# Hybrid attention, convolution and memory layer: one buffer for both parts of a transposed group, a third scan buffer, two gates on the score banks, two sums of squares in one, other loads and stores at the two ends

## The chip, the cores and the metric

The kernel runs on one core of a Trainium2 chip. The metric is the device time of one execution in microseconds (us), as the median of several runs. PE is the matrix engine (PEld its weight loads), DVE the vector engine, ACT the scalar engine, POOL the GpSimd engine, SP the engine that starts most DMA transfers. Matmuls read SBUF and write PSUM, which has eight banks of 128 x 512 floats; DVE and ACT read both memories, POOL and DMA are used on SBUF alone here.

## The reference

One layer, `x` of 1024 tokens by 1024 features, 256 memory tokens. Cut to what is computed:

```python
h = rmsnorm(x, g_in)
q, k, v, u, b, c, q_mem, gate = split(h @ w_in)       # 3584 columns
# stick-breaking attention, 8 heads of 64, strictly causal (s < t), no softmax
z = q @ k.T / 8
w = sigmoid(z) * prod over s < j < t of (1 - sigmoid(z[t, j]))
y_sb = w @ v
y_conv = b * causal_conv3(c * u)                      # 256 channels
m_k, m_v = split(rmsnorm(mem, g_mem) @ w_mem_kv)
y_mem = softmax(q_mem @ m_k.T / 8) @ m_v              # 4 heads of 64
y = concat(rmsnorm(y_sb), rmsnorm(y_conv), rmsnorm(y_mem))
x = x + (y * silu(gate)) @ w_out
out = rmsnorm(x, g_final)
```

## The kernel before

Tokens are held in reverse order, so that the product over later keys becomes a scan to the right. Everything that goes into a matmul is split into a high part in fp32r (a cast on ACT) and a low part (what the cast left, a subtraction on DVE or POOL), and a product is three matmuls (high by high, high by low, low by high), or two where one side is stacked.

The work, in the order in which it is written down:

- At the start `xT` comes in by eight row blocks (`xs`), is scaled by `g_in` (in `col`, the first DMA on SP) and split into `xh`, `xl`. Eight warming matmuls on a zero mask run first on PE, then the first half of the values and the projections of the first heads.
- `proj(n, ...)` makes 128 columns of a projection: weights loaded and split (`load_w`, tags `whi` and `wlo`, four half tiles each), 48 matmuls of 128 x 512 into two banks with tag `pj`, and for each bank an `evac`.
- `sb_head` is one attention head. For each pair of token blocks `scores` makes the scores in banks `z`, ACT takes two sigmoids of them, DVE scans the product (into a buffer `F`), and DVE or POOL multiplies the scan with the sigmoid into `sg`. `apply` transposes four blocks of `sg` on PE into a bank `tr`; `transposed` casts the bank to the high part (`wth`, ACT) and subtracts for the low part (`wtl`, DVE), and two matmuls by the values add up in a bank `av`.
- `mem_head` is one memory head: scores in a bank `z`, softmax with Exp on ACT, the same transposes.
- `stats(c)` sums the squares of one of the eight tiles `ys[c]` (two halves: a Square, the split, two matmuls by a column of ones, a copy, four small DMAs that turn the row into a column). Tiles 0 to 3 are attention, 4 and 5 convolution, 6 and 7 memory.
- `gate(c)` is a projection whose `evac` multiplies by the row scale (DVE), takes a Sigmoid (ACT, written back to the bank), multiplies with the tile (DVE or POOL) and ends with a multiplication that reads the bank again and writes `y` (DVE). Only this last one sets the bank free.
- The output product takes eight blocks of 128 tokens. Each has three groups of matmuls, for the convolution's tiles 4 and 5 (banks `pj`), the memory's 6 and 7 (banks `z`) and the attention's 0 to 3 (banks `tr`, `av`); DVE adds each, scaled by its group's rms, to `acc`. Then comes the final norm: a Square with a sum on ACT, a power on POOL, a scaling of one half on DVE and of the other on ACT, two stores on SP. The last block takes its last 512 columns in two pieces of 256.

No order is written by hand. The functions above only record operations with a priority; a planner (`Plan.lay_out`) then lays them on the five engines, by costs of its own, always taking the ready operation of least priority, and issues the instructions in that order. Projections are fillers of low urgency between the steps of attention. A tag with n buffers gives them out in the order in which its tiles were written down, and a buffer comes free when all users of its tile are done. `nc.either` lets the planner choose DVE or POOL. All instructions are issued by one line, so every row of the profile says L383, and rows are told apart by the names of tiles.

Of the kernel before, what the change touches and what calls it, by code (L numbers as in the profile page):

```python
# [24 lines left out]
F32 = mybir.dt.float32  # L25
F32R = mybir.dt.float32r
BF16 = mybir.dt.bfloat16
AF = mybir.ActivationFunctionType
ALU = mybir.AluOpType
AX = mybir.AxisListType  # L30

P = 128
# [354 lines left out]
def hymba_kernel(ctx, tc, xT, xr, wp, wv, memT, memr, wmem, cols, eye, wout, gfin, out):  # L387
# [6 lines left out]
    vyp = Pool(nc, "vyp", {"va": 1, "vb": 1, "y0": 1, "y1": 1})  # L394
    att = Pool(nc, "att", {"qh": 1, "ql": 1, "kh": 1, "kl": 1, "q": 2, "qs": 2, "k": 2, "sg0": 2, "sg1": 2, "F": 2, "wth": 3, "wtl": 2})
    small = Pool(nc, "small", {"avt": 1, "mx": 2, "sm": 2, "part": 2})
# [5 lines left out]
    def bank(tag):  # L402
        return psum.tile([P, H], F32, tag)
# [4 lines left out]
    def one(shape, dt, name):  # L408
        return const.tile(shape, dt, name, name)

    def f(ap):
# [35 lines left out]
    nc.vector.tensor_copy(ones, onesf)  # L447
    nc.sync.dma_start(out=col, in_=cols)
    warm = one([P, 2], F32, "warm")
# [14 lines left out]
    for k in range(KC):  # L464
# [5 lines left out]
        if k % 2 == 0:  # L470
            ws = stage([P, 2, 256])
            wh, wl = att.tile([P, 2, 256], F32R, "wth", "wsh"), att.tile([P, 2, 256], F32R, "wtl", "wsl")
            nc.sync.dma_start(out=ws, in_=wv[0, k // 2])
# [113 lines left out]

    def proj(n, evac, after=(), both=False):
        fills[0] += 1
        wh, wl = load_w(wp[n], [P, KC, P], 8.4 if fills[0] == 1 else None)  # L590
        ps = [bank("pj"), bank("pj")]
        steps = [(i, k) for i in range(2) for k in range(KC)]
        if both:

            steps = [(i, k) for k in range(KC) for i in range(2)]
        for i, k in steps:
            hf = HALVES[i]
            for a, (ww, xx) in enumerate(((wh, xh), (wh, xl), (wl, xh))):
                first = k == 0 and a == 0
                nc.tensor.matmul(ps[i], lhsT=ww[k], rhs=xx[k][:, hf], start=first,  # L600
                                 stop=(k == KC - 1 and a == 2), prio=FILL + fills[0] + (0 if both else 0.4 * i),
                                 after=after if first else ())
            if k == KC - 1:
                keep, nc.prio = nc.prio, EVAC + fills[0]
                evac(ps[i], hf)
                nc.prio = keep
# [6 lines left out]
    def transposed(blocks):  # L613

        tr = bank("tr")
        for i, blk in enumerate(blocks):
            nc.tensor.transpose(tr[:, i * P : (i + 1) * P], blk, ident)
        wh = att.tile([P, H], F32R, "wth")
        wl = att.tile([P, H], F32R, "wtl")
        n = len(blocks) * P  # L620
        nc.scalar.copy(wh[:, 0:n], tr[:, 0:n])
        nc.vector.tensor_tensor(wl[:, 0:n], tr[:, 0:n], f(wh[:, 0:n]), op=ALU.subtract)
        return wh, wl
# [9 lines left out]
    def scores(st, sp, b):  # L633
# [5 lines left out]
        for c0, c1 in ((lo, min(n, H)), (H, n)):  # L639
            if c1 <= c0:  # L640
                continue
            z = bank("z")
            m0 = c0 if c1 - c0 >= 256 else c1 - 256
            for s, qq in enumerate((st["q"], st["qs"])):
# [102 lines left out]

    def stats(c, late=False):


        keep, nc.prio = nc.prio, EVAC + 50
        g = 0 if c < 4 else 1 if c < 6 else 2
        part = small.tile([P, TB], F32, "part")
        for n, hf in enumerate(HALVES):

            s, hi, lo = ((att if late else stg).tile([P, H], dt, tag if late else "stg", "sq")
                         for dt, tag in ((F32, "F"), (F32R, "sg1"), (F32R, "sg1")))
            nc.scalar.activation(s, ys[c][:, hf], AF.Square)
            nc.scalar.copy(hi, s)
# [44 lines left out]

    def gate(c, after, both=False):
        def evac(ps, hf):
            gz, y = stage(), ys[c][:, hf]
            nc.vector.tensor_tensor(gz, ps, rb[:, hf], op=ALU.mult)
            nc.scalar.activation(ps, gz, AF.Sigmoid)
            nc.either.tensor_tensor(gz, gz, y, op=ALU.mult)  # L810
            nc.vector.scalar_tensor_tensor(y, ps, gout(c), gz, op0=ALU.mult, op1=ALU.mult)

        proj(16 + c, evac, after, both)

# [134 lines left out]
    stats(5, late=True)  # L949
    gate(5, ())  # L950
    stats(6, late=True)
    gate(6, (last[6],))
    stats(7, late=True)
    gate(7, (), both=True)
    nc.prio = POST
# [29 lines left out]
    for j in range(TB):  # L985
# [18 lines left out]
        for n, c0, c1 in todo:  # L1004
# [9 lines left out]
            if n == todo[-1][0]:  # L1014
                junk = att.tile([P, H], F32, "F", "junk")
                nc.scalar.activation(junk[:, 0 : c1 - c0], acc[:, c0:c1], AF.Square,
                                     accum_out=sj[:, c0 // 256 : c0 // 256 + 1])
                if c0 == 0:
                    nc.vector.tensor_tensor(acc[:, 0:H], acc[:, 0:H], gf[:, 0:H], op=ALU.mult)
# [5 lines left out]
        nc.vector.tensor_tensor(acc[:, H:], acc[:, H:], gf[:, H:], op=ALU.mult)  # L1025
        nc.vector.tensor_scalar(acc[:, HALVES[0]], acc[:, HALVES[0]], total, None, op0=ALU.mult)
        nc.scalar.activation(acc[:, HALVES[1]], acc[:, HALVES[1]], AF.Copy, scale=total)
        for hf in HALVES:
            nc.sync.dma_start(out=out[j][:, hf], in_=acc[:, hf])
    nc.emit()  # L1030
# [49 lines left out]
```

## Time and profile before

| what | value |
|---|---|
| time, median of 3 runs | 561.36 us (561.23 to 561.88) |
| time of the profiled execution | 565.04 us |
| its span, first to last instruction | 563.3 us |
| PE busy (matmuls) | 548.9 us, 97%, 2984 instructions |
| PEld busy (weight loads, beside the matmuls) | 468.1 us |
| DVE busy | 404.5 us, 72% |
| ACT busy | 359.7 us, 64% |
| POOL busy | 179.8 us, 32% |
| mean granted clock of PE | 0.996 |
| read from and written to HBM | 36.78 MB and 4.20 MB |

A row of the timeline has the start, the time taken, engine, line, operation, out<-in, the shape and, in brackets, the idle time of the engine before it and what ended that. The time of one matmul is from its start to the end of its drain, and the next one starts long before that end; what a matmul costs a PE that is never idle is the distance between two starts.

### The profile page before, as it was taken

How to read it: one execution, taken by the hardware profiler on the slowest of the kernel's cores; microseconds unless marked ns; L12 is line 12 of the kernel's file. 1: busy time of each engine (PE TensorE's matmuls, PEld its weight loads, DVE VectorE, ACT ScalarE, POOL GpSimd, SP SyncE). 2: the span in 40 equal slices, each digit the busy share in tenths (PEclk: the TensorE clock that was granted, in tenths of full speed). 3: DMA queues.
4: the chain of work that ended last, by engine and by line, in shares of the span. 5: the costliest groups of instructions: out<-in, count | busy, mean ns of one | idle time of the engine just before them, and what ended most of it. 6: DMA issues, size and time to landing. Idle time of an engine off the chain costs nothing.

```text
span 563.3 us, 8740 instructions
## 1 busy us (share of the span) xinstructions
PE 548.9 (97%) x2984; PEld 468.1 (83%) x2984; DVE 404.5 (72%) x657; ACT 359.7 (64%) x727; POOL 179.8 (32%) x214
## 2 busy tenths in 40 slices
PE   6999999999999999999999999999999999999995
PEld 4898789998888888888888868888888777888884
DVE  3354588879888898973487879667777877876674
ACT  4843478788786777683278787766589975332322
POOL 1130154225444432452053474331442108010010
PEclk9999999999999999999999999999999999999998
DMA  7962915052142710115742512342522342223302
GB/s 238 389 188 75 234 42 131 21 111 78 40 92 60 184 39 19 39 21 120 197 151 76 131 38 75 75 104 71 164 76 38 114 149 76 74 76 115 110 37 75
DMA packets 34688, 58.36 MB, mean 104 GB/s; under 512 B 13650, under 2 KB 14546, under 8 KB 34644
## 3 DMA queue, kind: packets, MB, share of 16 engines
q1 hardware_dynamic: 34644, 57.81, 36.7%
q8 instruction: 23, 0.38, 0.3%
q14 instruction: 21, 0.17, 0.1%
HBM read 36.78 MB, written 4.20 MB: 73 GB/s over the span
## 4 chain that ended last, share of the span: by engine, by line
PE 88%; DMA 3%; ACT 3%; issue 2%; DVE 2%; POOL 1%; SPq 0%; POOLq 0%; DVEq 0%; ACTq 0%
PE pj L383 50%; PE tr L383 15%; PE z L383 12%; PE av L383 11%; DMA xs<-in_xT 1%; DMA wraw<-in_wmem 1%; DMA q<-ql 1%; DVE stg L383 0%; ACT L383 0%; ACT vh L383 0%; DVE y L383 0%; POOL wlo L383 0%; ACT z L383 0%; ACT pj L383 0%; ACT whi L383 0%
## 5 line engine op out<-in xcount | busy, mean ns | idle before, releaser
L383 PE MATMUL pj<-xh,whi 128*128 128x512 f32 x352 | 139.4, 396 | 0.7 <-DVE y L383 0.7
L383 PE MATMUL pj<-xh,wlo 128*128 128x512 f32 x352 | 139.8, 397 | 0.0
L383 PE MATMUL pj<-xl,whi 128*128 128x512 f32 x352 | 139.4, 396 | 0.0
L383 POOL TENSOR_TENSOR sg<-sg,F 128x512 f32<-128x512 f32 (+5 forms) x60 | 62.0, 1041 | 74.3 <-DVE F L383 47.8
L383 PEld LDWEIGHTS pj<-xh,whi 128*128 128x128 f32 x352 | 66.2, 188 | 13.2 <-DVE y L383 1.0
L383 PEld LDWEIGHTS pj<-xh,wlo 128*128 128x128 f32 x352 | 66.2, 188 | 12.3 <-issue 0.3
L383 PEld LDWEIGHTS pj<-xl,whi 128*128 128x128 f32 x352 | 66.2, 188 | 12.1 <-issue 0.2
L383 ACT ACTIVATE sg<-z,rq 128x511 f32<-128x511 f32 (+2 forms) x96 | 55.9, 583 | 29.8 <-PE z L383 27.0
L383 POOL TENSOR_TENSOR wlo<-wraw,whi 128x512 fp32r<-128x512 f32 x36 | 48.3, 1343 | 83.3 <-ACT whi L383 71.4
L383 DVE TENSOR_TENSOR_SCAN F<-z,mask 128x512 f32<-128x512 f32 (+2 forms) x64 | 60.1, 947 | 13.1 <-ACT z L383 10.9
L383 DVE TENSOR_TENSOR wtl<-tr,wth 128x512 fp32r<-128x512 f32 (+1 forms) x96 | 58.8, 639 | 5.8 <-ACT wth L383 5.0
L383 ACT CAST wth<-tr 128x512 fp32r<-128x512 f32 (+1 forms) x96 | 49.4, 552 | 15.4 <-PE tr L383 14.8
L383 ACT ACTIVATE z<-z,nrq 128x512 f32<-128x512 f32 (+3 forms) x96 | 53.4, 557 | 2.3
L383 PE MATMUL tr<-ident,sg 128*128 128x128 f32 x288 | 48.9, 273 | 0.0
L383 ACT CAST whi<-wraw 128x512 fp32r<-128x512 f32 x56 | 34.1, 621 | 14.9 <-PE pj L383 11.1
L383 PE MATMUL av<-wth,vh 128*128 128x256 f32 (+1 forms) x160 | 42.7, 276 | 0.0
L383 PE MATMUL av<-wtl,vh 128*128 128x256 f32 (+1 forms) x160 | 41.4, 293 | 0.0
L383 PEld LDWEIGHTS tr<-ident,sg 128*128 128x128 f32 x288 | 34.6, 140 | 2.9 <-DVE sg L383 0.2
L383 ACT ACTIVATE junk<-acc 128x512 f32<-128x512 f32 (+1 forms) x17 | 10.3, 606 | 38.9 <-DVE acc L383 38.1
L383 DVE TENSOR_TENSOR_SCAN F<-z,F,mask 128x511 f32<-128x511 f32 (+1 forms) x32 | 32.3, 1009 | 3.0 <-ACT z L383 1.5
L383 PE MATMUL z<-k,q 128*128 128x512 f32 (+2 forms) x96 | 34.0, 356 | 0.4 <-DMA q<-ql 0.4
L383 PEld LDWEIGHTS av<-wth,vh 128*128 128x128 f32 x160 | 30.3, 189 | 3.3
(173 smaller groups left out, 1206.2 us busy)
## 6 DMA issues: line engine op xcount, KB each, us to landing
wraw<-in_wp SPq DMA_DIRECT2D x44, 256.0 KB, 3.0
rows<-in_xr SPq DMA_DIRECT2D x8, 512.0 KB, 8.5
acc<-in_xr SPq DMA_DIRECT2D x8, 512.0 KB, 3.3
out<-acc SPq DMA_DIRECT2D x16, 256.0 KB, 2.1
xs<-in_xT SPq DMA_DIRECT2D x6, 512.0 KB, 9.2
q<-qh SPq DMA_DIRECT2D x12, 256.0 KB, 3.0
q<-ql SPq DMA_DIRECT2D x12, 256.0 KB, 4.6
qs<-ql SPq DMA_DIRECT2D x12, 256.0 KB, 4.7
```

The lines of the kernel that those rows point to most:

```text
L383: f(*[real(x) for x in o.args], **{k: real(x) for k, x in o.kw.items()})
```

## The change

- `transposed` takes the high and the low part from one tile with tag `wt`, two buffers of 128 x 2 x 512. Before, the high part had three buffers (`wth`) and the low part two (`wtl`). The weights of the first values (`wsh`, `wsl`) move to the same tag.
- The scans' tag `F` has three buffers where it had two.
- `scores` no longer widens a stretch of 128 keys to 256. That stretch occurs once in each of the eight attention heads (the last pair of blocks, second block), with two matmuls.
- `stats` takes several tiles of one group: it adds the squares of the second to those of the first (DVE or POOL) and sends the sum through one split, one set of matmuls and one set of small DMAs. It is called for tiles 6 and 7 together, after tile 7 is there.
- `proj` and `gate` take a tag for their two banks; the gates of tiles 5 and 7 use `z`.
- `col` is loaded from ACT's queue instead of SP's.
- In the last block of the output the Square of the last 256 columns is a multiplication with a sum on DVE instead of an ACT operation, and the scaling and the stores are four pieces (256 columns DVE, 192 ACT, 256 DVE, 320 ACT), the last store issued by ACT.

```diff
-    att = Pool(nc, "att", {..., "F": 2, "wth": 3, "wtl": 2})
+    att = Pool(nc, "att", {..., "F": 3, "wt": 2})
...
-    nc.sync.dma_start(out=col, in_=cols)
+    nc.scalar.dma_start(out=col, in_=cols)
...
-            wh, wl = att.tile([P, 2, 256], F32R, "wth", "wsh"), att.tile([P, 2, 256], F32R, "wtl", "wsl")
+            wh, wl = pair_of(att.tile([P, 2, 2, 256], F32R, "wt", "ws"))
...
-    def proj(n, evac, after=(), both=False):
+    def proj(n, evac, after=(), both=False, tag="pj"):
...
-        ps = [bank("pj"), bank("pj")]
+        ps = [bank(tag), bank(tag)]
...
-        wh = att.tile([P, H], F32R, "wth")
-        wl = att.tile([P, H], F32R, "wtl")
+        wh, wl = pair_of(att.tile([P, 2, H], F32R, "wt"))
...
-            m0 = c0 if c1 - c0 >= 256 else c1 - 256
+            m0 = c0
...
-    def stats(c, late=False):
+    def stats(*cs, late=False):
...
-            nc.scalar.activation(s, ys[c][:, hf], AF.Square)
+            nc.scalar.activation(s, ys[cs[0]][:, hf], AF.Square)
+            if len(cs) > 1:
+                t = (att if late else stg).tile([P, H], F32, "F" if late else "stg", "sq")
+                nc.scalar.activation(t, ys[cs[1]][:, hf], AF.Square)
+                nc.either.tensor_tensor(s, s, t, op=ALU.add)
...
-    gate(5, ())
-    stats(6, late=True)
+    gate(5, (), tag="z")
+    stats(6, 7, late=True)
     gate(6, (last[6],))
-    stats(7, late=True)
-    gate(7, (), both=True)
+    gate(7, (), both=True, tag="z")
...
-                nc.scalar.activation(junk[:, 0 : c1 - c0], acc[:, c0:c1], AF.Square,
-                                     accum_out=sj[:, c0 // 256 : c0 // 256 + 1])
+                if c1 - c0 < H and c1 == D:
+                    nc.vector.scalar_tensor_tensor(junk[:, 0 : c1 - c0], acc[:, c0:c1], 1.0, acc[:, c0:c1], op0=ALU.mult,
+                                                   op1=ALU.mult, accum_out=sj[:, c0 // 256 : c0 // 256 + 1])
+                else:
+                    nc.scalar.activation(junk[:, 0 : c1 - c0], acc[:, c0:c1], AF.Square,
+                                         accum_out=sj[:, c0 // 256 : c0 // 256 + 1])
...
-        nc.vector.tensor_scalar(acc[:, HALVES[0]], acc[:, HALVES[0]], total, None, op0=ALU.mult)
-        nc.scalar.activation(acc[:, HALVES[1]], acc[:, HALVES[1]], AF.Copy, scale=total)
-        for hf in HALVES:
-            nc.sync.dma_start(out=out[j][:, hf], in_=acc[:, hf])
+        for n, c in enumerate((slice(0, 256), slice(H, H + 192), slice(256, H), slice(H + 192, D)) if j == TB - 1 else HALVES):
+            if n % 2:
+                nc.scalar.activation(acc[:, c], acc[:, c], AF.Copy, scale=total)
+            else:
+                nc.vector.tensor_scalar(acc[:, c], acc[:, c], total, None, op0=ALU.mult)
+            (nc.scalar if n == 3 else nc.sync).dma_start(out=out[j][:, c], in_=acc[:, c])
```

Since tags, costs and banks feed the planner, the order changes on all engines. Three places matter for the prediction.

On PE, at the passage from the last gate to the output product, before: `pj_5336` is the second bank of the last gate (tile 7), `z_5412` and `z_5421` are banks of the group of tiles 6 and 7, `tr_5430` and `tr_5433` those of the attention's group, `pj_5451` the first bank of tiles 4 and 5, which takes over a bank of the last gate.

```order
L383 MATMUL pj_5336<-xh_448,wlo_5187 128x512
L383 MATMUL z_5412<-woh_5368,yh_4860 128x512
...
L383 MATMUL z_5421<-woh_5368,yl_4885 128x512
L383 MATMUL tr_5430<-woh_5398,yh_4860 128x512
L383 MATMUL tr_5433<-woh_5398,yh_4860 128x512
...
L383 MATMUL tr_5433<-woh_5426,yh_4860 128x512
L383 MATMUL pj_5451<-woh_4721,yh_4860 128x512
```

The same place in the changed program: `z_5223` is now the last gate's second bank, `z_5348` the first of the output product that takes over a bank of that gate.

```order
L383 MATMUL z_5223<-xh_444,wlo_5159 128x512
L383 MATMUL pj_5296<-woh_4631,yh_4767 128x512
...
L383 MATMUL pj_5309<-woh_5233,yl_4791 128x512
L383 MATMUL tr_5322<-woh_5272,yh_4767 128x512
...
L383 MATMUL tr_5338<-wol_5311,yh_4767 128x512
L383 MATMUL z_5348<-woh_5244,yh_4767 128x512
```

Between the last gate's last matmul and the first one that needs a bank of that gate stood 14 matmuls; now there are 24.

On PE at the gates before that, in the changed program: `z_5123` is the second bank of tile 5's gate, `pj_5001` the second bank of tile 6's, `z_5185` the first of tile 7's, `av_5183` the sums of squares.

```order
L383 MATMUL z_5123<-xh_444,wlo_4741 128x512
L383 MATMUL pj_5001<-xh_404,wlo_4930 128x512
L383 MATMUL pj_5001<-xh_444,whi_4921 128x512
L383 MATMUL pj_5001<-xl_453,whi_4921 128x512
L383 MATMUL pj_5001<-xh_444,wlo_4930 128x512
L383 MATMUL av_5183<-sq_5168,ones_99 2x512
L383 MATMUL z_5185<-xh_121,whi_5039 128x512
```

Before, the gates of tiles 3, 5, 6 and 7 followed each other on the same two `pj` banks; now tile 6's gate runs ahead of tile 5's, and 21 matmuls stand between the end of `z_5123` and the first matmul of the bank that takes over from it. The four `pj` matmuls at the end of tile 6's gate come late, after all of tile 5's.

On DVE the end of the program before (`acc` the last block, `ssf` the sums):

```order
L383 SCALAR_TENSOR_TENSOR acc_5914<-av_6086,rg_4451,acc_5914 128x256
L383 TENSOR_TENSOR ssf_5520<-ssf_5520 128x1
L383 TENSOR_TENSOR acc_5914<-acc_5914,gf_5134 128x512
L383 TENSOR_SCALAR acc_5914<-acc_5914,ssf_5520 128x512
L1075 UNCONDITIONAL_BRANCH
```

And after:

```order
L383 SCALAR_TENSOR_TENSOR acc_5790<-av_5962,rg_4366,acc_5790 128x256
L383 SCALAR_TENSOR_TENSOR junk_5981,ssf_5402<-acc_5790 128x256
L383 TENSOR_TENSOR ssf_5402<-ssf_5402 128x1
L383 TENSOR_TENSOR acc_5790<-acc_5790,gf_4988 128x512
L383 TENSOR_SCALAR acc_5790<-acc_5790,ssf_5402 128x256 x2
```

The last sum of squares now stands on DVE between the last addition and the total, and the scaling is two pieces. SP then has three stores instead of two, and ACT ends with a DMA of 128 x 320.

More of the change, by code (lines that the diff above doesn't have):

```diff
@@ L394, in hymba_kernel @@
     vyp = Pool(nc, "vyp", {"va": 1, "vb": 1, "y0": 1, "y1": 1})
-    att = Pool(nc, "att", {"qh": 1, "ql": 1, "kh": 1, "kl": 1, "q": 2, "qs": 2, "k": 2, "sg0": 2, "sg1": 2, "F": 2, "wth": 3, "wtl": 2})
+    att = Pool(nc, "att", {"qh": 1, "ql": 1, "kh": 1, "kl": 1, "q": 2, "qs": 2, "k": 2, "sg0": 2, "sg1": 2, "F": 3, "wt": 2})
     small = Pool(nc, "small", {"avt": 1, "mx": 2, "sm": 2, "part": 2})
@@ L409, in one, with pair_of @@
         return const.tile(shape, dt, name, name)
+    def pair_of(t):
+        return t[:, 0], t[:, 1]
     def f(ap):
@@ L746, in hymba_kernel @@
     summed = set()
-    def stats(c, late=False):
+    def stats(*cs, late=False):
         keep, nc.prio = nc.prio, EVAC + 50
-        g = 0 if c < 4 else 1 if c < 6 else 2
+        g = 0 if cs[0] < 4 else 1 if cs[0] < 6 else 2
         part = small.tile([P, TB], F32, "part")
@@ L803, in stacks, with gate @@
         return dst
-    def gate(c, after, both=False):
+    def gate(c, after, both=False, tag="pj"):
         def evac(ps, hf):
@@ L811, in evac @@
             nc.vector.scalar_tensor_tensor(y, ps, gout(c), gz, op0=ALU.mult, op1=ALU.mult)
-        proj(16 + c, evac, after, both)
+        proj(16 + c, evac, after, both, tag)
     def conv(cc):
```

## The prediction

> **What bounds the kernel now.** I read the page first, then PE's busy time by stretches, then the waits of PE, then the timeline at each wait. From the page:
>
> ```profile
> PE 548.9 (97%) x2984; PEld 468.1 (83%) x2984; DVE 404.5 (72%) x657; ACT 359.7 (64%) x727; POOL 179.8 (32%) x214
> PE   6999999999999999999999999999999999999995
> PE 88%; DMA 3%; ACT 3%; issue 2%; DVE 2%; POOL 1%; SPq 0%; POOLq 0%; DVEq 0%; ACTq 0%
> ```
>
> PE is busy 548.9 of 563.3 us; of 40 slices only the first and the last are short, and 88% of the chain that ended last is PE. The same by stretches, PE alone:
>
> ```profile
> 0.00:9.00 9.00, 3.59 (x8) 1.00 0.64 177
> 9.00:13.00 4.00, 3.92 (x18) 1.00 0.93 353
> 13.00:325.00 312.00, 311.63 (x1838) 1.00 0.41 111
> 325.00:336.00 11.00, 10.31 (x50) 1.00 0.17 48
> 336.00:440.00 104.00, 104.00 (x554) 1.00 0.33 82
> 440.00:475.00 35.00, 33.65 (x151) 1.00 0.43 136
> 475.00:557.00 82.00, 81.79 (x373) 1.00 0.22 77
> ```
>
> Outside the start (5.4 us idle before 9.0) and the end (nothing after 557), PE is idle for 0.37 us up to 325, 0.69 in 325 to 336 and 1.35 in 440 to 475. So a change has four ways to pay: less work on PE, an earlier first matmul, fewer of those small holes, a shorter tail. What it takes off ACT, DVE, POOL or SP is worth nothing unless PE or the tail waits for it. The waits of PE, and one of ACT that I use later:
>
> ```profile
> PE tr L383 <- ACT xh L383: 4.2, 1, 4.2
> PE pj L383 <- DVE y L383: 1.4, 2, 0.7
> PE pj L383 <- POOL wlo L383: 0.4, 1, 0.4
> ACT wth L383 <- PE tr L383: 14.8, 24, 2.6
> ```
>
> **The change part by part.** *Narrower scores.* Eight heads have one stretch of 128 keys, with two matmuls that were 256 wide. First 256 wide, then the nearest 128 wide pair, in `av`:
>
> ```profile
> 116.87 0.28 PE L383 MATMUL pj<-wlo,xh 128*128 128x256 f32 x1
> 116.99 0.28 PE L383 MATMUL z<-k,q 128*128 128x256 f32 x1
> 117.11 0.28 PE L383 MATMUL z<-k,qs 128*128 128x256 f32 x1
> 161.38 0.22 PE L383 MATMUL av<-wth,vh 128*128 128x128 f32 x1
> 161.43 0.28 PE L383 MATMUL av<-wtl,vh 128*128 128x128 f32 x1
> 161.55 0.30 PE L383 MATMUL tr<-ident,sg 128*128 128x128 f32 x1
> ```
>
> From start to start a 256 wide one takes 0.12 us, a pair 0.24. The 128 wide pair takes 0.05 and 0.12, together 0.17. So 8 x 0.07 = 0.55 us less; bounds 0 (if both take the 0.12) and 8 x 0.14 = 1.1 (if both take the 0.05). I take 0.55, the row of the same two widths on the same weights. The Trainium skill, in "TensorE: Matmul & The Clock Gate", section "LDWEIGHTS (loading the stationary operand)", speaks against this edit: a weight load takes its columns divided by 1.2 in ns, 107 ns for 128 columns, so a stream with a load for each matmul would not go below that however narrow the data. The row agrees in its second matmul (0.12) and not in its first (0.05). By that rule the pair would take 0.21, the edit 0.2 us, and the sum below would be 0.35 us higher.
>
> *Sums of squares of tiles 6 and 7 together.* One of eight `stats` goes: four matmuls by the ones, and on ACT, DVE or POOL and SP two casts, two copies, two subtractions and eight small DMAs, against two additions more.
>
> ```profile
> 453.46 0.39 PE L383 MATMUL av<-sq,ones 128*2 128x512 f32 x1
> 453.68 0.39 PE L383 MATMUL pj<-xl,whi 128*128 128x512 f32 x1
> ```
>
> One costs PE 0.22 us, four 0.9 us. The rest is beside PE. The sum is complete later than tile 6's alone was, but 42 of tile 7's gate's matmuls and then 24 of the output product stand before the first result that its scale multiplies; cover gone, it would cost about the 2 us that a small DMA takes, and I cost it at nothing.
>
> *Gates of tiles 5 and 7 on the score banks.* Both waits for `y` are a `pj` bank that a gate's last multiplication had not yet read:
>
> ```profile
> 448.52 0.47 PE L383 MATMUL pj<-xh,wlo 128*128 128x512 f32 x1
> 449.69 0.50 PE L383 MATMUL pj<-xh,whi 128*128 128x512 f32 x1 [0.69 <-DVE y L383]
> 446.23 1.28 ACT L383 ACT_TABLE_LOAD   x1
> 468.26 0.39 PE L383 MATMUL pj<-xh,wlo 128*128 128x512 f32 x1
> 471.43 0.39 PE L383 MATMUL tr<-woh,yh 128*128 128x512 f32 x1
> 472.48 0.50 PE L383 MATMUL pj<-woh,yh 128*128 128x512 f32 x1 [0.66 <-DVE y L383]
> ```
>
> From start to start 1.17 and 1.05 us went by where 0.23 is usual (471.43 less 468.26 is 14 such steps), so the holes cost 0.94 and 0.82, together 1.76 us. The second: the last gate's last matmul ends its step at 468.49 and its bank was free 4.0 us later, with 14 matmuls (3.2 us) to cover it. In the new order 24 stand there, 24 x 0.226 = 5.4 us. The first came at 31 instructions (6.5 us) after the bank's last matmul, so it needed 7.5 us: ACT was changing its table between Exp and Sigmoid, 1.28 us each, in between. In the new order tile 6's banks are not needed until the output product, over 40 matmuls later; the tightest place is now tile 7's second bank, 21 matmuls or 4.75 us after tile 5's gate ends, with Exp done by then. I take both holes as gone, 1.76; bounds 0 and 2.0 (with the slow step behind each).
>
> *The column loaded by ACT.*
>
> ```profile
> 0.74 0.39 SPq L383 DMA_DIRECT2D col<-in_cols  x1
> 1.18 0.42 SPq L383 DMA_DIRECT2D stg<-in_wv  x1
> 8.52 0.91 ACT L383 ACTIVATE xh<-xs,col 128x256 fp32r<-128x256 f32 x2 [6.30 <-DMA xs<-in_xT]
> 9.08 1.01 PE L383 MATMUL tr<-wsh,xh 128*128 128x256 f32 x3 [4.23 <-ACT xh L383]
> 12.45 0.41 PE L383 MATMUL av<-wsl,xh 128*128 128x256 f32 x1
> 12.66 0.41 PE L383 MATMUL av<-wsh,xh 128*128 128x256 f32 x1
> ```
>
> Everything that SP loads is issued 1.18 - 0.74 = 0.44 us earlier. The first real matmul waits for `xh`, that for `xs`, so PE starts 0.44 us earlier if the transfers keep their pace; bounds 0 (the transfers, not their issue, decide) and 0.44. I take 0.44, as PE has no hole between 13 and 60 that a late load would fill. ACT issues one DMA ahead of its table load and is idle for 6.3 us there.
>
> *The tail.*
>
> ```profile
> 556.83 0.48 DVE L383 SCALAR_TENSOR_TENSOR acc<-av,rg,acc 128x256 f32<-128x256 f32 x1 [0.16 <-PE av L383]
> 557.95 0.16 DVE L383 TENSOR_TENSOR ssf<-ssf 128x1 f32<-128x1 f32 x1 [0.63 <-ACT junk L383]
> 559.15 0.72 ACT L383 ACTIVATE acc<-acc,ssf 128x512 f32<-128x512 f32 x1 [1.23 <-POOL ssf L383]
> 559.15 0.48 DVE L383 TENSOR_SCALAR acc<-acc,ssf 128x512 f32<-128x512 f32 x1 [0.44 <-POOL ssf L383]
> 559.66 0.81 SPq L383 DMA_DIRECT2D out<-acc  x2
> out<-acc SPq DMA_DIRECT2D x16, 256.0 KB, 2.1
> ```
>
> The Square on ACT takes 0.64 us from the end of the addition (557.31) to the total (557.95); on DVE I put it at the 0.48 of the row above it and a gap of 0.06, 0.1 us less (bounds 0 and 0.2). The pieces: a 256 wide scaling ends about 0.2 us sooner, so the first store goes out at some 559.45 instead of 559.66. But three stores in a row on SP, at 0.40 each, put the third at 560.25, where the second stood at 560.06. ACT's own store follows 0.72 and one more start-up of work, at about 560.1. Stores are smaller, and how much of the 2.1 us is size the trace does not tell. I take the pieces at nothing, bounds -0.3 and +0.3.
>
> *Buffers.* The third `F` is beside PE: no wait of PE or of the tail names a scan. The common `wt` costs the high part its third buffer: a cast on ACT must now wait until PE has read the low part of two groups before, and everything behind it on ACT waits too. In the trace 24 casts wait, all for the transposes (14.8 us in all), none for a buffer, and PE is not idle for any of them. In the new order the nearest reuse leaves 1.6 us of matmuls from the last read of a buffer to the first matmul that uses its next content; from the end of the transposes to that matmul both orders go as low as 1.1 us, and in the trace PE did not wait there. So I cost it at nothing, with the mixing of attention and projections as its cover. But the whole order is laid anew, and it will have holes of its own: the ones not named above stay as they are in my sum, and I add 0.4 us for one more of the size of `POOL wlo`. Bounds -0.7 (the 325 to 336 hole closes) and +2.
>
> **Sum.** -0.55 - 0.9 - 1.76 - 0.44 - 0.1 + 0.4 = -3.35 us, against the profiled execution's 565.04 us (span 563.3 and 1.7 around it), so 561.7 with a profile. The median of 561.36 is 3.7 lower than that execution; the terms are distances on PE and in the tail, and carry over: 558.0 us.
>
> **The rivals.** *The hole moves to tile 7's gate.* If emptying the bank of tile 5's gate takes the 7.5 us seen at 449.69 instead of the 4.0 seen at 472.48, the 4.75 us of cover are 2.75 short, and the forecast becomes 558.0 + 2.75 = 560.8, within 0.2% of before. For it: the chain is the same four steps, and four Sigmoids of two gates now follow each other on ACT. Against it: no Exp is left to change tables for. Chance 0.15.
>
> *The slow stretch of PE does not move.* Between 9.08 and 12.9 PE's 256 wide matmuls start 0.21 us apart, later 0.12, though the clock row says 1.00. If that ends at a fixed moment and not a fixed time after PE's start, the 0.44 us are worth about half, and the time is 558.2. The Trainium skill says so: "TensorE: Matmul & The Clock Gate", section "What's actually happening", has a gate at half rate that is released by free-running windows of about 3.4 us, wherever the kernel starts. The trace agrees with the half rate and a length of 3.8 us; whether the end moves it can't show. Chance 0.15.
>
> *Slower: ACT blocked by the transposed pairs.* 96 groups go through `wt`. If each high cast that waits for its buffer delays PE by over (3.35 + 1.1) / 96 = 0.05 us, all of the gain is gone and the kernel is slower by over 0.2%; at 0.1 us each the time is 558.0 + 9.6 = 567.6. For it: ACT is 64% busy and takes its work in order. Against it: the planner knows the two buffers and has put other matmuls in between. Chance 0.06.
>
> **How the numbers follow.** The forecast has 0.60, the rivals 0.15, 0.15 and 0.06, something not thought of 0.04. I count as the same what lies within 0.2% (1.1 us), about what a measurement of this kernel can tell. Faster: 0.60 + 0.15 + 0.06 of the first rival and the unknown = 0.81; same 0.13; slower 0.06. Range: all bounds at their good ends would give 561.36 - 1.1 - 0.9 - 2.0 - 0.44 - 0.5 - 0.7 = 555.7, which is unlikely at once; I take 556.2. Upwards it takes in most of the first rival: 560.6.
>
> **What would show it.** Right: no wait of PE for `y` in the gates; 28 matmuls by the ones and 16 scores 128 wide with pairs near 0.17; the first real matmul near 8.6; PE busy near 545. Wrong: new rows of PE waiting for `y`, `wt` or `sg`, above all at tile 7's gate, or ACT waiting for PE's `av` before casts of `wt`; a first matmul still at 9.1; a last store that lands over 3.2 us after the power.

## The result, and the profile after

The changed kernel takes 557.79 us, median of 7 runs (557.62 to 560.05). The kernel before, run beside it on the same chip, takes 561.88 us, median of 7 (561.23 to 564.65). The ratio is 0.9932 [0.9918, 0.9946]: faster by 0.7%. The profiled execution took 558.57 us, its span is 556.8 us, the mean granted clock 0.996.

From the page of the changed kernel, its span, the busy times, PE's busy tenths in 40 slices and the shares of the chain that ended last:

```profile
span 556.8 us, 8701 instructions
PE 546.4 (98%) x2980; PEld 466.6 (84%) x2980; DVE 405.0 (73%) x659; ACT 351.7 (63%) x718; POOL 183.2 (33%) x214
PE   9899999999999999999999999999999999999995
PE 90%; DMA 4%; issue 2%; ACT 2%; SPq 1%; DVE 1%; POOLq 0%; POOL 0%; ACTq 0%
```

It is the same picture, with 2.5 us less of PE and a first slice that is full. PE's busy time by stretches, in the changed kernel (stretch, its length, busy time and matmuls, granted clock, DMA share, GB/s):

```profile
0.00:9.00 9.00, 7.75 (x35) 1.00 0.74 204
...
13.00:325.00 312.00, 309.73 (x1822) 1.00 0.41 110
325.00:336.00 11.00, 10.86 (x49) 1.00 0.27 72
336.00:440.00 104.00, 104.00 (x558) 1.00 0.35 92
440.00:475.00 35.00, 35.00 (x156) 1.00 0.34 99
```

The 1.35 us of idle PE in 440 to 475 are gone, and so is most of the 0.69 in 325 to 336. In 13 to 325 PE is now idle for 2.27 us where it was for 0.37, and 5.4 idle us of the first nine became 1.25. Both show in the kernel before too, when it is profiled a second time: see the first experiment. All the waits of PE in the changed kernel (us in total, times, longest):

```profile
PE tr L383 <- DVE onesf L383: 1.3, 1, 1.3
PE tr L383 <- ACT xh L383: 1.1, 1, 1.1
PE tr L383 <- DVE xl L383: 0.8, 1, 0.8
PE z L383 <- DMA q<-ql: 0.3, 1, 0.3
```

No wait for `y` is left, none for `wlo` and none for `sq`. How near the last gate still comes to one shows in the first of the two multiplications that set its banks free (DVE's timeline) and the first matmul that takes over a bank of that gate (PE's):

```profile
467.19 0.75 DVE L383 SCALAR_TENSOR_TENSOR y<-z,col,stg 128x512 f32<-128x512 f32 x1 [1.19 <-POOL stg L383]
```

```profile
468.16 0.39 PE L383 MATMUL z<-woh,yh 128*128 128x512 f32 x1
```

The gate's last matmul ends its step at 462.72, the multiplication ends at 467.94, and the matmul starts at 468.16: of 5.4 us of cover 5.2 were needed. At tile 7's gate it is 4.2 of 4.8 us (tile 5's gate ends its step at 450.44, its bank is read for the last time until 454.62, the matmul that takes it over starts at 455.24). The waits for `xh` and `xl` are these, on PE's timeline of the changed kernel:

```profile
22.12 0.39 PE L383 MATMUL pj<-xh,w 128*128 128x512 f32 x1
23.64 0.50 PE L383 MATMUL tr<-ws,xh 128*128 128x256 f32 x2 [1.14 <-ACT xh L383]
24.96 0.39 PE L383 MATMUL tr<-ws,xl 128*128 128x256 f32 x1 [0.82 <-DVE xl L383]
```

There PE has caught up with the loading of `xT`. The scores of 128 keys, and all matmuls by the ones (number, shortest, median and longest in ns, first and last start), in the changed kernel:

```profile
88.16 0.22 PE L383 MATMUL z<-k,q 128*128 128x128 f32 x1
88.22 0.28 PE L383 MATMUL z<-k,qs 128*128 128x128 f32 x1
88.34 0.33 PE L383 MATMUL pj<-wlo,xh 128*128 128x256 f32 x1
```

```profile
L383 PE MATMUL av<-sq,ones x28: 389/396/473, 121.0 to 452.9; 128*2 128x512 f32 x28
```

A pair takes 0.06 and 0.12 (0.060 and 0.115 before rounding, and about so for seven of the eight), and 28 matmuls by the ones are left of 32. The tail of the changed kernel, DVE, POOL, ACT and the stores:

```profile
550.13 0.48 DVE L383 SCALAR_TENSOR_TENSOR acc<-av,rg,acc 128x256 f32<-128x256 f32 x1 [0.15 <-PE av L383]
550.65 0.42 DVE L383 SCALAR_TENSOR_TENSOR junk<-acc 128x256 f32<-128x256 f32 x1
551.12 0.16 DVE L383 TENSOR_TENSOR ssf<-ssf 128x1 f32<-128x1 f32 x1
552.32 0.91 ACT L383 ACTIVATE acc<-acc,ssf 128x192 f32<-128x192 f32 x2 [2.53 <-POOL ssf L383]
552.32 0.61 DVE L383 TENSOR_SCALAR acc<-acc,ssf 128x256 f32<-128x256 f32 x2 [0.44 <-POOL ssf L383]
552.70 1.31 SPq L383 DMA_DIRECT2D out<-acc  x3
553.25 0.35 ACTq L383 DMA_DIRECT2D out<-acc  x1
```

The last addition to the total is 0.99 us (551.12 less 550.13) where it was 1.12 (557.95 less 556.83). But from the start of the scaling to the last landing it is 3.47 us (552.32 to 555.79, the third store of SP) where it was 3.21 (559.15 to 562.36).

### The profile page after: what moved, and what is told of

The parts are those of the page before. It is cut to its first block, busy times and chain, and to the rows that moved or that the text cites. A ratio compares the mean times of both kernels' runs of the same rounds, so it can differ in the third digit from the quotient of the medians.

```text
span 556.8 us, 8701 instructions
## 1 busy us (share of the span) xinstructions
PE 546.4 (98%) x2980; PEld 466.6 (84%) x2980; DVE 405.0 (73%) x659; ACT 351.7 (63%) x718; POOL 183.2 (33%) x214
## 4 chain that ended last, share of the span: by engine, by line
PE 90%; DMA 4%; issue 2%; ACT 2%; SPq 1%; DVE 1%; POOLq 0%; POOL 0%; ACTq 0%
PE pj L383 49%; PE z L383 16%; PE tr L383 15%; PE av L383 10%; DMA xs<-in_xT 2%; DMA stg<-in_wv 1%; DMA q<-ql 1%; SPq L383 1%; ACT vh L383 0%; ACT whi L383 0%; DVE xl L383 0%; ACT z L383 0%; ACT xh L383 0%; ACT kh L383 0%; POOLq L1087 0%
## 5 line engine op out<-in xcount | busy, mean ns | idle before, releaser
L383 PE MATMUL pj<-xh,wlo 128*128 128x512 f32 x320 | 127.3, 398 | 0.0
L383 PE MATMUL pj<-xl,whi 128*128 128x512 f32 x320 | 127.2, 398 | 0.0
L383 PE MATMUL pj<-xh,whi 128*128 128x512 f32 x320 | 126.6, 396 | 0.0
L383 POOL TENSOR_TENSOR sg<-sg,F 128x511 f32<-128x511 f32 (+5 forms) x60 | 64.3, 1078 | 75.4 <-DVE F L383 43.9
L383 PEld LDWEIGHTS pj<-xh,wlo 128*128 128x128 f32 x320 | 60.2, 188 | 10.8 <-issue 0.2
L383 DVE TENSOR_TENSOR wt<-tr,wt 128x512 fp32r<-128x512 f32 (+1 forms) x96 | 58.8, 638 | 9.3 <-ACT wt L383 8.4
L383 ACT CAST wt<-tr 128x512 fp32r<-128x512 f32 (+1 forms) x96 | 49.7, 553 | 17.6 <-PE tr L383 17.2
L383 PE MATMUL av<-wt,vh 128*128 128x256 f32 (+1 forms) x320 | 58.9, 285 | 0.0
L383 PEld LDWEIGHTS av<-wt,vh 128*128 128x128 f32 x320 | 49.6, 189 | 5.5 <-DVE wt L383 0.4
L383 PE MATMUL z<-k,qs 128*128 128x512 f32 (+2 forms) x96 | 32.6, 341 | 0.0
```

The source lines that it names most:

```text
L383: f(*[real(x) for x in o.args], **{k: real(x) for k, x in o.kw.items()})
```

## The experiments

Each was timed beside the kernel before. To compare single executions I cut the span in three, from PE's timeline: the start of the first real matmul, the time from there to the last matmul's start, the tail. The middle one is cut again. For each matmul the usual step of its shape (0.226 us for 128x512, 0.118 for 128x256 and so on) is taken from the distance to the next start; what is over is "lost", by place, and the rest is the work:

| kernel (one profiled execution) | first matmul | first to last | tail | work | lost to 60 | 60 to 320 | 320 to 340 | 340 to 435 | 435 to 480 |
|---|---|---|---|---|---|---|---|---|---|
| before, first profile | 9.08 | 547.43 | 6.75 | 523.6 | 2.4 | 13.0 | 2.5 | 3.2 | 2.5 |
| before, again | 4.96 | 549.46 | 6.75 | 523.6 | 4.8 | 12.4 | 2.5 | 3.2 | 2.6 |
| changed | 4.64 | 545.17 | 6.97 | 522.0 | 4.5 | 12.7 | 1.8 | 3.4 | 0.45 |
| gates alone | 5.17 | 547.01 | 6.74 | 523.6 | 3.4 | 12.4 | 2.6 | 3.9 | 0.8 |
| changed, gates on `pj` | 4.57 | 547.50 | 6.97 | 522.1 | 3.9 | 12.8 | 1.8 | 3.4 | 3.3 |
| less work alone | 5.16 | 550.65 | 6.75 | 521.6 | 5.2 | 13.5 | 1.9 | 5.6 | 2.8 |
| buffers alone | 5.14 | 548.83 | 6.74 | 523.5 | 3.7 | 12.7 | 2.3 | 3.8 | 2.7 |
| changed, old buffers | 4.32 | 547.38 | 6.97 | 521.6 | 4.8 | 13.0 | 2.0 | 4.9 | 0.9 |

The usual step of a 128 wide matmul depends on what follows it, so where the order is another, up to 0.5 us moves between "work" and "lost"; kernels with other buffers are compared by "first to last". Most of the 12 to 13 us in 60 to 320 come from that choice too: with the median of the shape as the usual step, 2.0 to 2.8 us are left there.

What varies between executions of one program lies nearly all in the first 60 us. So a second reading takes from "first to last" what is lost by matmuls that start before 65 us (usual step here the median of the shape in the kernel before: 0.227, 0.175, 0.120 and 0.108 us for 512, 384, 256 and 128 columns, 0.233 for the sums of squares). It keeps the work and all losses after the start, and is called the later part:

| kernels, one profiled execution each | later part |
|---|---|
| before: first profile, again, with the column on ACT | 544.84, 545.11, 545.16 |
| gates alone | 544.10 |
| less work alone | 545.35 |
| buffers alone | 545.60 |
| gates and less work | 543.08 |
| changed with old buffers: four pieces, two halves | 543.09, 543.14 |
| changed: as it is, column on SP, two halves by SP, two halves by SP and ACT | 541.13, 541.13, 541.12, 541.11 |
| changed, gates on `pj` | 544.05 |

Kernels that differ only in the column or in the end agree within 0.1 us (within 0.3 with the first profile of before), so a difference of 0.5 us is read better here than in medians whose intervals are 1.5 to 2.3 us wide.

**The kernel before, profiled again.** No edit.

> The kernel before, unchanged, for a second profile of its start. Theory A (the moment at which the first block of xT lands varies from execution to execution, whatever queue loads the column): PE's first real matmul may lie anywhere between about 4.6 us (seen in the changed kernel's profile) and 9.1 us (seen in the first profile of before), and the time moves with it. Theory B (the column at the head of SP's queue holds up what follows): it starts near 9.1 us again. Under A the fast executions of before, 561.3, are those that start near 5 us, so an early start here would come with about 561.5, and a late one with about 565.

562.98 us, span 561.2; 17 runs of the kernel before, beside it, have a median of 561.9 (560.70 to 563.74). The first real matmul, from the timeline of PE, in this execution, and two of PE's waits:

```profile
4.96 1.01 PE L383 MATMUL tr<-wsh,xh 128*128 128x256 f32 x3
```

```profile
PE tr L383 <- ACT xh L383: 1.3, 1, 1.3
...
PE tr L383 <- DVE xl L383: 0.8, 1, 0.8
```

PE starts 4.12 us earlier than in the first profile, and at 22 to 25 us it waits for `xh` and `xl` as the changed kernel does. So the hole at the start of the first profile (the first `xs` landed at 8.43 us, here at 4.32) was that execution's own: it cost 4.12 us and gave 2.0 of them back, since data that PE reached later had come in meanwhile (the middle part is 547.43 against 549.46). So 2.1 of the 3.7 us between that profile and the median were its late start; the other 1.6 (562.98 less 561.36) are within the scatter of the 17 runs. Nothing in them has to be a price of profiling. All further comparisons are with this execution.

**The column alone.** The kernel before with one line changed:

```diff
-    nc.sync.dma_start(out=col, in_=cols)
+    nc.scalar.dma_start(out=col, in_=cols)
```

> The kernel before with one line changed: the column is loaded from ACT's queue. Theory A: the issue of all else is 0.44 us earlier and that is all: 0 to 0.5 us faster, 561.0 to 561.5, with the same scatter of starts. Theory B: the first matmul moves from 9 to under 5 us in every execution, and most of that or at least 2 us shows in the time: under 559.5.

561.27 us (560.25 to 562.9, 12 runs), ratio 0.9987 [0.9974, 1.0000]. In its profile:

```profile
1.18 1.37 SPq L383 DMA_DIRECT2D xs<-in_xT  x3
4.50 0.80 PE L383 MATMUL tr<-wsh,xh 128*128 128x256 f32 x2
```

`xs` is issued at 1.18 instead of 1.65, lands at 3.85 instead of 4.32, and the first real matmul is at 4.50 instead of 4.96: the whole 0.46 arrives at PE. The Trainium skill, "DMA: Bandwidth & Descriptors", section "Issuing engines are not separate DMA queues", says that starting transfers on several engines saves only the time of starting them; that is what is seen here, 0.46 us of it.

That one pair of executions agrees so well is in part chance. Over all profiles the first real matmul is at 4.96 to 5.17 us in six executions with the column on SP (the late first profile left out) and at 4.32 to 4.97 in seven with it on ACT, 5.12 and 4.58 on average. In the time the gain is not clear of the noise.

**The changed kernel without that line.** The same edit taken back:

> The changed kernel with the column back on SP's queue. Theory A: 558.0 to 558.3, at most 0.5 us above the changed kernel's 557.8. Theory B: 2 us or more above it, over 559.8, and a first matmul near 9 us in the profile.

558.32 us (557.51 to 559.21, 6 runs), ratio 0.9943 [0.9925, 0.9961], against 0.9932 with it: 0.6 us, the same size as alone, and again less than the intervals are wide. In its profile PE starts at 5.13 (changed: 4.64).

**The changed kernel with the old end of two halves, both stored by SP.** The Square on DVE stays:

```diff
-        for n, c in enumerate((slice(0, 256), ..., slice(H + 192, D)) if j == TB - 1 else HALVES):
...
+        nc.vector.tensor_scalar(acc[:, HALVES[0]], acc[:, HALVES[0]], total, None, op0=ALU.mult)
+        nc.scalar.activation(acc[:, HALVES[1]], acc[:, HALVES[1]], AF.Copy, scale=total)
+        for hf in HALVES:
+            nc.sync.dma_start(out=out[j][:, hf], in_=acc[:, hf])
```

> The changed kernel with the scaling and the stores of the last block as before (two halves of 512 columns, both stores on SP); the Square of the last 256 columns stays on DVE. By the changed kernel's trace the last store landed 3.47 us after the scaling began, against 3.21 before, and six store semaphores were waited for at the end. If the four pieces are what cost that, this one is 0.2 to 0.4 us faster than the changed kernel: 557.5. If the difference is only how busy HBM was, it is the same within 0.1 us. By my prediction (pieces worth nothing) it is the same.

557.37 us (556.88 to 560.08, 6 runs), ratio 0.9933 [0.9913, 0.9953]. Its end, from the timeline:

```profile
552.70 0.49 DVE L383 TENSOR_SCALAR acc<-acc,ssf 128x512 f32<-128x512 f32 x1 [0.44 <-POOL ssf L383]
553.22 0.81 SPq L383 DMA_DIRECT2D out<-acc  x2
```

The last landing is at 555.92, 3.22 us after the scaling starts. The tail is 6.62 us, against 6.97 with four pieces and 6.75 before (6.74 to 6.75 in the seven profiles with the end of before, 6.97 in four with four pieces, 6.62 in three with the Square on DVE and two halves): the Square on DVE saves 0.13, the four pieces cost 0.35 (0.25 until the last landing, 0.1 between that and the end of the span). The first store does go out earlier (0.38 us after the scaling starts instead of 0.52), but SP then needs until 0.86 us past it to send its third, and that third still takes 2.23 us to land (553.56 to 555.79), where the second half took 2.32. In the time this is not clear of the noise: the ratio is 0.9933, that of the changed kernel 0.9932.

**The two gates on the scores' banks alone.** In the kernel before, `proj` and `gate` get the `tag`, and:

```diff
-    gate(5, ())
+    gate(5, (), tag="z")
...
-    gate(7, (), both=True)
+    gate(7, (), both=True, tag="z")
```

> The kernel before with only the banks of two gates changed (tiles 5 and 7 on the score banks). Theory of the prediction (the two holes of PE in 440 to 475 are the gates' banks): PE loses nothing there any more, 1.8 to 2.1 us faster than before, ratio 0.9965. Rival (the holes came from the way this one order fell, and any new order would close them): also about 2 us here, so this run alone does not tell them apart; the next one does. If the hole moves to tile 7's gate (4.97 us of matmuls there by the order), a new wait for y appears and the gain is under 1 us.

560.86 us (559.77 to 563.36, 12 runs; before beside it 562.04, 35 runs), ratio 0.9972 [0.9953, 0.9990]. No wait for `y` is left in it. Its largest wait of PE in the later part is

```profile
PE pj L383 <- POOL wlo L383: 0.7, 2, 0.5
```

of which 0.5 us is at 426. By the ratio the edit alone gains 1.6 us (0.6 to 2.6). In the trace the two holes of 1.87 us (1.05 and 0.82 in the profile taken again) are gone, and 0.7 more is lost in 340 to 435, at that wait for `wlo`; the later part is 1.0 us shorter.

**The changed kernel with all gates on `pj`.** The same two lines taken back:

> The changed kernel with all gates back on the projection banks. Theory of the prediction: both holes are back, 1.8 us or more slower than the changed kernel, 559.5 and above. Rival (any new order closes them): at most 0.5 us slower, and PE in its profile without a wait for y between 430 and 475. By the order, tile 7's gate has only 3.6 us of matmuls to cover its bank here, the output product 5.2, so I expect one hole of up to 1 us at the first and none at the second: 558.5.

561.35 us (560.2 to 563.07, 12 runs), ratio 0.9980 [0.9961, 0.9999]. From PE's timeline in this kernel:

```profile
437.79 0.40 PE L383 MATMUL pj<-xh,wlo 128*128 128x512 f32 x1
440.06 0.50 PE L383 MATMUL pj<-xh,whi 128*128 128x512 f32 x1 [1.87 <-DVE y L383]
```

With everything else of the change, the hole at the gates' banks is 2.04 us (440.06 - 437.79 - 0.23), larger than the 1.05 before, and a second of 0.49 follows at 468.6. The edit is worth 2.7 us here by the ratios (0.48% of 562) and 2.9 by the later part, against 1.6 and 1.0 alone: the two holes are 2.53 us together where they were 1.87. The rival, that any new order closes them, is out. My own figure of 558.5, reckoned from 3.6 and 5.2 us of cover, was too low: 5.2 us were not enough at the output product either.

**Less work alone.** The narrow scores and the common `stats(6, 7)` in the kernel before:

```diff
-            m0 = c0 if c1 - c0 >= 256 else c1 - 256
+            m0 = c0
...
-    stats(6, late=True)
+    stats(6, 7, late=True)
...
-    stats(7, late=True)
```

> The kernel before with the narrower scores and the common sums of squares of tiles 6 and 7 alone. PE has four matmuls of 0.23 less and eight pairs of 0.07 less: 1.45 us faster by work alone, ratio 0.9974. If the new order also closes the holes of 440 to 475 (4.07 and 5.65 us of matmuls at the two places), up to 3.4 us faster. Rival: a common sum comes later and something waits for it: no gain.

562.76 us (562.08 to 564.82, 12 runs), ratio 1.0009 [0.9992, 1.0027]: nothing. By count PE has 1.45 us less to do. The waits that have grown after the start are at the gates' banks:

```profile
PE pj L383 <- DVE y L383: 2.3, 3, 0.8
```

```profile
434.68 0.49 PE L383 MATMUL av<-wtl,mv 128*128 128x512 f32 x1
436.00 0.50 PE L383 MATMUL pj<-xh,whi 128*128 128x512 f32 x1 [0.83 <-DVE y L383]
```

Three holes of 1.10, 0.94 and 0.82 us stand where there were two of 1.05 and 0.82: one more microsecond. Matmuls taken away from between a gate's end and the next use of its bank do not shorten the time in which the bank is emptied. Small steps between 340 and 435 are longer too; why, the trace does not show. Together they use up the cut work: the later part is 0.2 us longer than before. The rival, that something waits for the common sum, is not seen (PE's wait for `sq` is 0.2 us, as before). The profiled execution took 564.35 us, near the upper end of its runs; 1.2 us of that are a slow stretch at 25 us (last section).

**The buffers alone.** The tags `F` and `wt` and the two uses of `pair_of` in the kernel before:

```diff
-    att = Pool(nc, "att", {..., "F": 2, "wth": 3, "wtl": 2})
+    att = Pool(nc, "att", {..., "F": 3, "wt": 2})
```

> The kernel before with one tag for both parts of a transposed group (two buffers) and three scan buffers alone. Theory of the prediction: nothing by itself, within 0.5 us of before, apart from what the new order does to the holes of 440 to 475 (4.07 and 5.2 us of matmuls there): with these closed, 1 to 2 us faster. Rival (ACT is held up by casts that wait for their buffer): slower by 1 us or more, with new waits of PE for wt and of ACT for av.

563.39 us (562.24 to 566.24, 12 runs), ratio 1.0024 [1.0004, 1.0045]: 1.3 us slower. Waits of PE that the profile of before did not have, or had smaller:

```profile
PE av L383 <- DVE sq L383: 0.8, 2, 0.5
...
PE av L383 <- ACT stg L383: 0.3, 1, 0.3
PE av L383 <- ACT wt L383: 0.2, 1, 0.2
PE av L383 <- DVE wt L383: 0.2, 1, 0.2
```

The largest, 0.5 us at 447.7, is at the last set of sums of squares, which in this order came due before DVE had split the squares. With `stats(6, 7)` in the full change there is one set less, and no such wait. The waits for `y` are shorter here (0.9 us, 1.5 before), and this execution, 562.49, is at the low end of its kernel's runs: its later part is 0.5 us longer than before, and the rest of the 1.3 us the trace does not show. The theory of the prediction, within 0.5 us of before, did not hold in the median; the rival's slowdown came, but of its sign, waits for `wt`, there are only 0.4 us.

**The changed kernel with the old buffers.** The same lines taken back:

> The changed kernel with the buffers as before (three of wth, two of wtl, two of F). The buffers alone measured 0.24% slower than before. Theory C (the shared buffer costs something of its own): this one is faster than the changed kernel by about 1 us, 556.8. Theory D (the buffers only shift where the order leaves holes at the gates' banks, and with the gates on the score banks those are closed): the same as the changed kernel within 0.5 us, 557.3 to 558.3.

560.19 us (558.99 to 560.75, 7 runs), ratio 0.9959 [0.9942, 0.9976]. In the company of the other edits the buffers *gain*: 0.27% or 1.5 us by the ratios (whose intervals just touch), 2.2 us by PE's middle part (547.38 against 545.17), 2.0 by the later part. Neither theory stated for this run gave that. The one place that can be named, from PE's timeline:

```profile
432.91 0.49 PE L383 MATMUL av<-wtl,mv 128*128 128x512 f32 x1
433.57 0.50 PE L383 MATMUL pj<-xh,whi 128*128 128x512 f32 x1 [0.16 <-DVE y L383]
```

A gate's bank again, 0.43 us lost, and 0.12 in the step behind it. Two more steps lose 0.39 and 0.31 us (330.0 and 326.8), where the changed kernel loses 0.18 and 0.17 nearby. That is 0.9 us; the remaining 1.3 us are spread over many steps that are longer by 0.1 us or less. No run has the third `F` without the common `wt`, or the other way round, and none keeps the order and changes the room: which of the two buffers gains, and whether by its room or only by another order, stays open.

**The changed kernel with two halves, the second stored by ACT.** As in the run with the old end, and:

```diff
+        for n, hf in enumerate(HALVES):
+            (nc.scalar if n and j == TB - 1 else nc.sync).dma_start(out=out[j][:, hf], in_=acc[:, hf])
```

> The changed kernel with the last block stored in two halves again, the second one issued by ACT instead of SP. By the traces the distance from the start of PE's last matmul to the end was 6.75 us before, 6.97 with four pieces, 6.62 with two halves on SP. SP's second store went out 0.38 us after its first; ACT's can go out as soon as its scaling ends, 0.72 us after the power, about 0.15 us sooner. Expected 6.45 to 6.5 us for that distance, a time 0.4 to 0.5 us under the changed kernel: 557.3. If the last landing hangs on HBM and not on the issue, 6.6 us.

556.86 us (556.44 to 558.24, 6 runs), ratio 0.9908 [0.9890, 0.9926], the fastest of all that were measured; its interval overlaps that of the changed kernel. Its end:

```profile
551.11 0.72 ACT L383 ACTIVATE acc<-acc,ssf 128x512 f32<-128x512 f32 x1 [2.53 <-POOL ssf L383]
551.86 0.36 ACTq L383 DMA_DIRECT2D out<-acc  x1
```

The store of ACT lands at 554.33, 3.22 us after the scaling starts, just as the second store of SP did. It did go out 0.15 us sooner (0.75 us after the scaling starts, SP's 0.90), as expected, but took 2.46 us to land instead of 2.32, so the 0.1 to 0.15 us expected from it are missing. The tail is 6.62 in both. So two halves are worth 0.35 us over four pieces, and which engine sends the second half makes no difference in the profile. What its median has over the run with the old end (0.5 us) is not explained by the tail; PE's loss up to 60 us is 1.0 us smaller in its profile, the part that varies from one execution to the next.

**Gates and less work together.** The kernel before with the edits of the two runs above, the gates' banks and less work (so the changed kernel without its buffers, its column and its end):

> The kernel before with the gates on the score banks, the narrower scores and the common sums of squares, and nothing else. Separately the gates measured 0.28% faster and the two cuts of work nothing. If a cut of work only pays when the gates' banks no longer stop PE, the two together give their sum and the 1.45 us of work: 1.6 + 1.4 = 3 us, ratio 0.9946. If the parts simply add as measured, 1.1 us, ratio 0.998.

559.86 us (559.71 to 560.28, 6 runs), ratio 0.9957 [0.9941, 0.9973]: 2.4 us. Alone the gates gave 1.6 and the work nothing. That the parts add as measured, 0.998, is outside the interval; the full sum of 3 us, 0.9946, is inside. By the later part the same work adds 0.2 us alone and takes off 1.0 behind the gates (543.08 against 544.10). With the bank free in time, the cut work is worth about 1 us of its 1.45.

**The old buffers with the end of two halves.** The fastest version, with the buffers of before:

> All that has measured or read as a gain: gates on the score banks, less work, the column on ACT's queue, the last Square on DVE, two halves with the second store on ACT, and the buffers as before. Expected 0.4 us under the kernel with the old buffers and four pieces, and 0.4 to 1.4 us under the changed kernel: 556.4 to 557.4, ratio to before 0.990 to 0.9925.

559.49 us (558.63 to 561.44, 7 runs), ratio 0.9955 [0.9934, 0.9975], against 0.9908 [0.9890, 0.9926] with the new buffers. The intervals do not meet, PE's middle part is 546.41 against 544.20, again 2.2 us. The two were timed beside the same runs of before. That the buffers pay within this change is shown twice by the traces and here by the medians too, and this version was a wrong guess.

## Why the prediction was right, point by point

The forecast was 558.0 us, the measured median 557.79; faster was right. Part of the closeness is luck. The forecast was a gain of 3.35 us on a median of 561.36; measured beside each other, the gain is 4.1 us on 561.88. By the two executions with a like start (before again, and changed), the span of 561.18 loses 4.39 us, and the terms are:

- *Narrow scores and the common sum of squares*, forecast -0.55 and -0.9: the work of PE is 1.6 us less by the table, 1.45 by count. The pairs take 0.06 and 0.115 us as the row in `av` had said. The floor of 107 ns that I drew from the time of a load holds for the second matmul of a pair and not for the first, so the two together are well under the 0.21 reckoned from it. But "the rest is beside PE" is only true where the gates' banks are free in time: alone the same edits gave nothing, and behind the gates about 1 us.
- *The gates on the scores' banks*, forecast -1.76: the loss from 435 to 480 went from 2.61 to 0.45 us, -2.16. Both holes are gone, and the first rival (the hole moves to tile 7's gate) with them: no wait for `y` is left anywhere, so 4.75 us of cover were enough (4.2 were needed). At the output product I reckoned with 4.0 us to empty the bank and 5.4 of cover. It took 5.2, so the hole is closed as forecast, but with 0.2 us to spare and not 1.4: the margin was lucky.
- *The column*, forecast -0.44: 0.46 in its own run, 0.54 between the averages of all profiles. The first real matmul, expected near 8.6, is at 4.64, since the 9.08 it was reckoned from was that of a late start.
- *The tail*, forecast -0.1 with the pieces at nothing: +0.22. The Square gave its 0.13. The step that failed is the pieces, +0.35, just past the bound of +0.3: I had the third store on SP issued 0.2 later than the second had been, and let the smaller size make that good. Counted from the start of the scaling it was 0.35 later (1.24 against 0.89), and its size saved 0.1. My sign for it being wrong, a last landing over 3.2 us after the power, came true (3.47).
- *Holes of the new order*, forecast +0.4: the stretch 320 to 340 lost 0.74 less, the others between 0 and 435 changed by +0.2 together. The term had the wrong sign; the bound of -0.7 named the very stretch.
- *Buffers*, forecast 0: wrong in kind. By the ratios they are worth +1.3 alone and -1.5 to -2.6 in company, by the later part +0.5 and -2.0. My argument looked for a cast that waits for its buffer. The traces show another order with small losses in other places, a gate's bank among them; why it is better in company stays open. The rival in which ACT is blocked by the transposed pairs did not come: PE waits nowhere for `wt` in the changed kernel.
- *The slow stretch at the start*: the rival would have halved the column's gain. The column's run shows 0.46 at the first matmul and 0.6 in the medians, so there is no sign of a loss; a half of 0.44 is too little for these intervals to exclude.
- *Reading the base*: I took the 3.7 us between the profile and the median as an overhead that carries over. 2.1 us of it were a late start of 4.1 us, half of it given back, the rest scatter. No term was hurt by it, as each is a distance, but "PE has no hole between 13 and 60" was true of that execution alone.

So two terms were too pessimistic (the gates by 0.4, the new holes by 0.9) and one too optimistic (the tail by 0.3): the sum of -3.35 was about 1 us short of these two executions and 0.7 short of the medians. That the forecast comes within 0.2 us of the time is luck, as the kernel before, too, measured 0.5 us more beside it. What the sum, read from one finished order, could not have is that its edits do not add: the ratios of the four edits timed alone (column, gates, work, buffers) come to -0.45 us together; all of them, with the new ends, to -3.8. By the later part gates, work and buffers alone give -1.0, +0.2 and +0.5, and -4.0 together.

## What to carry to other kernels

Before a cut of work is priced, find the wait that its removal exposes: here 1.4 us less of matmuls was worth nothing until the bank that a slow evacuation holds was taken out of the way, and then about 1 us. Where a planner lays the order anew, an edit timed alone can have the other sign in company, so time the change with one edit taken back as well as each edit alone. And profile a base twice before a difference between its profile and its median is explained.

## What the runs showed of the hardware

With the same program the first block of `xT` landed 8.43 us after the start of the span in one execution and 4.32 in another, so the first 10 us of one profile say little.

How long PE runs at half rate is a matter of the execution, too. In the run with less work alone, the holes at 22 to 25 us were followed by thirteen steps of 0.21 us instead of 0.12, from PE's timeline:

```profile
25.71 0.42 PE L383 MATMUL tr<-wsh,xh 128*128 128x256 f32 x1
25.92 0.41 PE L383 MATMUL tr<-wsl,xh 128*128 128x256 f32 x1
...
28.27 0.37 PE L383 MATMUL av<-wsh,xh 128*128 128x256 f32 x1
28.48 0.28 PE L383 MATMUL av<-wsl,xh 128*128 128x256 f32 x1
```

That is 1.2 us more. The trace's record of the granted clock has it at half from 25.05 to 28.46 us, for 3.41 us. PE by stretches, granted clock in the column behind the busy time, first of that run and then of the changed kernel:

```profile
25.00:30.00 5.00, 4.67 (x25) 0.66 0.92 309
```

```profile
25.00:30.00 5.00, 5.00 (x33) 1.00 0.94 280
```

The changed kernel had the like holes there (1.14 and 0.82 us) and no slow steps. And at the start, two executions whose first real matmul was at 5.13 and 5.16 us (the changed kernel without the column's line, and less work alone) left the half rate at about 7.2 us and by 5.8 us at the latest. By the clock records of all the traces the full rate begins between 3.96 and 7.19 us in the thirteen executions whose first real matmul is at 4.3 to 5.2 us, and at 12.92 in the one that started at 9.08. So the end of the slow stretch is tied neither to the start of the work nor to a fixed moment. The Trainium skill, "TensorE: Matmul & The Clock Gate", section "What's actually happening", has the window of some 3.4 us run freely, wherever the work starts; these runs agree in that.
